# Infinity norm of 8192 rows: other load widths in the last eighth of the work

## The chip, the cores and the metric

The kernel runs on one core of a Trainium2 chip. The metric is the device time of one execution in microseconds (us). The kernel before took 626.63 us (median of three runs, 626.33 to 626.69).

## The reference

The input is a float32 matrix of 8192 rows and 8192 columns, 268.44 MB. The output is, for each row, the largest absolute value in it:

```
return np.linalg.norm(x, ord=np.inf, axis=1)
```

Every element is read once from HBM and compared once. Nothing else is computed.

## The kernel before

**Division of the work.** Each of the 128 partitions handles 64 whole rows. A *tile* is two rows for each partition: 128 x 16384 elements, 8.39 MB. A partition's two rows lie next to each other in HBM, so its 16384 elements are contiguous there. There are 32 tiles. The first 24 are the *bulk* (loop at L300 to L307): one load for each tile, issued on SyncE's queue at L303, and one reduction on VectorE, which gives both rows' maxima at once, into `r_bulk`. Three tile buffers (`BUFS=3`) rotate, so the load of a tile waits until VectorE has finished the tile three before it.

**The tail.** The last eight tiles are cut into several loads each, so that VectorE can start on a part of a tile as soon as that part has landed. `TAIL` (L18) holds the widths, in elements of a partition, of the loads of the first seven tail tiles; the loop at L309 to L320 issues them at L315. A reduction may not mix two rows, so `segments` (L39) cuts a load that crosses column 8192 of its tile into two reductions. Their results go to columns of `part`.

**The last tile.** `LAST` (L29) is the list of loads of the eighth tile, each a row (0 or 1) and a width, in the order of issue (L341). All but the last load of each row are reduced into single columns of the tile `t` itself, which stand just behind the place where that row's last load is put; the last reduction of a row reads its last load and these columns together, and writes `r_tail` (L345). After the first load of this list, one small reduction folds `part` into `r_tail` (L353).

**The end.** The store of `r_bulk` is issued on ScalarE's queue (L357) after the third-last load's reduction. The store of `r_tail` is issued on SyncE's queue (L359) behind the last reduction.

**Order and waits.** SyncE issues all loads in program order. A load waits for its buffer, as said. Loads also take turns on eight completion semaphores, so a load waits for the landing of the load eight before it where this isn't implied by its other wait. VectorE's reductions run in program order; each waits for its load's landing. All reductions show in the profile under line L296, the helper `absmax`.

**Sums of the widths.** Before, the seven tiles in `TAIL` are 20 loads and 26 reductions, and `LAST` is 12 loads and 12 reductions. With the small reduction over `part` that is 32 loads and 39 instructions on VectorE in the tail.

Of the kernel before, what the change touches and what calls it, by code (L numbers as in the profile page):

```python
# [15 lines left out]


TAIL = [  # L18
    [12672, 3712],
    [4992, 11392],  # L20
    [7040, 9344],
    [9344, 7040],
    [3584, 6784, 6016],
    [3968, 4224, 4736, 3456],
    [4096, 3584, 3200, 2944, 2560],
]


LAST = (  # L29
    [(0, w) for w in (2176, 1792, 1792, 1664)]  # L30
    + [(1, w) for w in (1664, 1408, 1280, 1152, 1024, 896)]
    + [(0, 768), (1, 768)]
)


# [359 lines left out]
```

## Time and profile before

| | |
|---|---|
| time, three runs | 626.33, 626.63, 626.69 us |
| the profiled execution | span 624.1 us, from the first load's issue to the end; the page gives no other time for it |
| median of the runs less this span | 2.5 us, outside the span |
| VectorE busy | 552.4 us, 89% of the span |
| DMA | 268.44 MB read, a mean of 430 GB/s |
| last tail load issued | 611.38 us after the span's start |
| last reduction ends, store of `r_tail` issued | 623.28 us, 623.31 us |

The profile is one execution on the chip. Its page names engines PE (TensorE), DVE (VectorE), ACT (ScalarE), POOL (GpSimd) and SP (SyncE); a trailing q means the engine's instruction queue, where DMAs are issued. The rows of instruction groups have busy time and the mean of one instruction in ns, then idle time just before them and what ended it. Consecutive reductions overlap by somewhat under 0.1 us in the records, so the time that one adds is read from start to start.

### The profile page before, as it was taken

To read this page: it belongs to the slowest core of one execution; us is meant where nothing else is said; L and a number is where in the kernel's file an instruction comes from. 1 tells how busy PE (TensorE), PEld (TensorE's weight loads), DVE (VectorE), ACT (ScalarE), POOL (GpSimd) and SP (SyncE) were. 2 spreads that over 40 slices of the span, in tenths; PEclk is the share of its full clock that TensorE was granted. 3 is DMA by queue.
4 is the path that set the end of the run, shared out by engine and by line. 5 is a ranking of instruction groups with operands and counts; after the bars stand their busy time and mean duration, and the time that the engine had idled before them with its cause. 6 is when DMAs were issued, how large, how long until landed. Compare 5 with 4: busy or idle time off the path is not lost.

```text
span 624.1 us, 151 instructions
## 1 busy us (share of the span) xinstructions
DVE 552.4 (89%) x63; POOL 0.3 (0%) x5
## 2 busy tenths in 40 slices
DVE  0688988889988899888898888988889999999999
POOL 0000000000000000000000000000000000000000
DMA  9999999999999999999999999999999999999998
GB/s 403 470 403 454 420 428 445 403 470 403 470 403 441 433 403 470 403 470 403 470 403 470 403 462 412 437 437 403 470 434 397 440 448 422 422 437 430 429 427 354
DMA packets 8593, 268.47 MB, mean 430 GB/s; under 512 B 1424, under 2 KB 1424, under 8 KB 2832
## 3 DMA queue, kind: packets, MB, share of 16 engines
q1 hardware_dynamic: 8064, 268.44, 99.7%
q10 hardware_dynamic: 528, 0.02, 0.1%
q14 instruction: 1, 0.01, 0.0%
HBM read 268.44 MB, written 0.03 MB: 430 GB/s over the span
## 4 chain that ended last, share of the span: by engine, by line
DMA 63%; DVE 36%; another core or an unknown queue 0%; DVEq 0%; issue 0%
DMA t<-in_x_dram 63%; DVE r_bulk L296 25%; DVE part L296 8%; DVE t L296 3%; DVEq L390 0%; DVE r_tail L296 0%
## 5 line engine op out<-in xcount | busy, mean ns | idle before, releaser
L296 DVE TENSOR_REDUCE r_bulk<-t 128x2 f32<-128x16384 f32 x24 | 413.3, 17220 | 70.6 <-DMA t<-in_x_dram 70.6
L296 DVE TENSOR_REDUCE part<-t 128x1 f32<-128x8192 f32 (+19 forms) x26 | 121.3, 4741 | 0.3
L296 DVE TENSOR_REDUCE t<-t 128x1 f32<-128x1792 f32 (+7 forms) x10 | 16.3, 1692 | 0.0
L296 DVE TENSOR_REDUCE r_tail<-t 128x1 f32<-128x772 f32 (+1 forms) x2 | 1.8, 948 | 0.0
L296 DVE TENSOR_REDUCE r_tail<-part 128x14 f32<-128x42 f32 x1 | 0.2, 192 | 0.0
L293 POOL MEMSET part<- 128x42 f32 x1 | 0.1, 133 | 0.0
L379 POOL MEMSET const-bfloat16-1.0<- 128x1 bf16 x1 | 0.1, 101 | 0.0
L379 POOL MEMSET const-uint8-127<- 128x1 uint8 x1 | 0.1, 101 | 0.0
L379 POOL MEMSET const-float32-0.0<- 128x1 f32 x1 | 0.1, 98 | 0.2 <-issue 0.2
L379 POOL MEMSET const-float32-1.0<- 128x1 f32 x1 | 0.1, 98 | 0.0
## 6 DMA issues: line engine op xcount, KB each, us to landing
t<-in_x_dram SPq DMA_DIRECT2D x2, 4672.0 KB, 37.5
t<-in_x_dram SPq DMA_DIRECT2D x2, 3520.0 KB, 36.2
t<-in_x_dram SPq DMA_DIRECT2D x1, 6336.0 KB, 36.3
t<-in_x_dram SPq DMA_DIRECT2D x1, 5696.0 KB, 40.5
t<-in_x_dram SPq DMA_DIRECT2D x2, 1792.0 KB, 34.3
t<-in_x_dram SPq DMA_DIRECT2D x1, 3392.0 KB, 37.5
t<-in_x_dram SPq DMA_DIRECT2D x1, 3008.0 KB, 44.2
t<-in_x_dram SPq DMA_DIRECT2D x1, 2496.0 KB, 27.3
```

The source lines that it names most:

```text
L293: nc.gpsimd.memset(part[:], 0.0)
L296: return nc.vector.reduce_max(out=o, in_=i, axis=X, apply_absolute_value=True)
L379: nc = _bacc.Bacc("TRN2", target_bir_lowering=False, num_devices=1)
```

## The change

Only the two lists of widths change. In `TAIL` the number of loads stays 20; two tiles are now cut at the end of a row (8192, 8192), and of the others five still have one load that crosses it, so the reductions go from 26 to 25. `LAST` has 11 loads instead of 12, wider at the start, with the rows in another order; its two final loads are 896 and 768 wide instead of 768 and 768. In all: 31 loads and 37 instructions on VectorE.

```
 TAIL = [
-    [12672, 3712],
-    [4992, 11392],
-    [7040, 9344],
-    [9344, 7040],
-    [3584, 6784, 6016],
-    [3968, 4224, 4736, 3456],
-    [4096, 3584, 3200, 2944, 2560],
+    [8192, 8192],
+    [12032, 4352],
+    [8192, 8192],
+    [7808, 8576],
+    [3584, 6272, 6528],
+    [5376, 4736, 3712, 2560],
+    [4096, 3712, 3200, 2688, 2688],
 ]

 LAST = (
-    [(0, w) for w in (2176, 1792, 1792, 1664)]
-    + [(1, w) for w in (1664, 1408, 1280, 1152, 1024, 896)]
-    + [(0, 768), (1, 768)]
+    [(0, 2432), (0, 2176), (1, 1920), (1, 1792), (0, 1536), (1, 1408)]
+    + [(1, 1280), (0, 1152), (1, 1024), (0, 896), (1, 768)]
 )
```

## The prediction

> **What bounds the kernel now.** I read the page first: engines, slices, groups.
>
> ```profile
> DVE 552.4 (89%) x63; POOL 0.3 (0%) x5
> DMA  9999999999999999999999999999999999999998
> ...
> L296 DVE TENSOR_REDUCE r_bulk<-t 128x2 f32<-128x16384 f32 x24 | 413.3, 17220 | 70.6 <-DMA t<-in_x_dram 70.6
> L296 DVE TENSOR_REDUCE part<-t 128x1 f32<-128x8192 f32 (+19 forms) x26 | 121.3, 4741 | 0.3
> ```
>
> The DMA engines are full from end to end. In the bulk, VectorE waits for every load (70.6 us in all); in the tail it hardly waits (0.3 us). That doesn't make VectorE the bound: it was given a backlog. So next come the busy times of two stretches, tail and bulk (length, VectorE busy, number of instructions), and the chain of waits in the tail (start, length, what).
>
> ```profile
> 466.66:622.20 155.54, 155.26 (x39) 0.00 (x0) 1.00 0.99 426
> 41.03:466.66 425.63, 378.83 (x22) 0.00 (x0) 1.00 1.00 433
> ```
>
> ```profile
> 501.18 34.55 DMA t<-in_x_dram
> 535.73 0.02 issue
> 535.75 17.35 DVE part L296 x3
> 553.10 0.02 issue
> 553.12 34.71 DMA t<-in_x_dram
> 587.83 0.02 issue
> 587.85 17.52 DVE part L296 x6
> 605.37 2.33 DVE t L296
> 607.70 0.10 DVE r_tail L296
> 607.80 13.50 DVE t L296 x9
> 621.30 0.17 issue
> 621.47 0.76 DVE r_tail L296
> ```
>
> VectorE is busy for 155.26 of 155.54 us, and twice the chain goes through a load that lands just as VectorE gets to it (535.73 and 587.83). So both are the bound at once. The last load is issued at 611.38 and takes 10.8 us to land (row of that load in the DMA issues): 622.2. The timeline shows the last reduction behind it:
>
> ```profile
> 621.47 1.81 DVE L296 TENSOR_REDUCE r_tail<-t 128x1 f32<-128x772 f32 x2
> 621.59 0.41 ACTq L357 DMA_DIRECT2D out_dram<-r_bulk  x1
> 623.31 0.35 SPq L359 DMA_DIRECT2D out_dram<-r_tail  x1
> ```
>
> The first of the pair starts at 621.47. An instruction of 772 elements takes 772/0.96 = 0.80 us and a fixed part of 0.06 (below), so the second starts at 622.34, about 0.15 after its load landed and with no gap behind the first. VectorE is the later of the two by 0.15 us. That is the most that any relief of VectorE can bring; beyond it the loads hold the end.
>
> **What a load costs.** The second and the 24th bulk reduction start 0.02 after their loads' landing, at 41.05 and 466.68: 425.63/22 = 19.35 us for a tile in one load. The eight tail tiles, in 32 loads, take 622.2 - 466.66 = 155.5; in eight loads they would take 154.8. So 24 extra loads cost 0.75 us, 0.03 each. One load less: -0.03 us, and the last landing is at about 622.15. Crossing a row's end costs the queue nothing: the 12672-wide load lands 14.9 after the one before (445.24 + 36.3 against 466.66), 1.18 ns an element, and the bulk load has 19.35/16384 = 1.18. So cutting at the row's end doesn't change the stream.
>
> **What a reduction costs.** By shape, 8192 elements take a mean of 8681 ns and 1152 take 1346: 7335/7040 = 1.042 ns an element and 146 ns fixed. Start to start it is less: the 8192-wide reduction that starts at 483.82 is followed by 4480 and 3712, and the next starts at 501.06: 17.24 us, of which 16384/0.96 = 17.07 is elements, so 0.06 fixed for each. Two instructions less (one in `part`, one in the last tile): -0.12 us of VectorE.
>
> **Where VectorE waits.** Loads' landings at the ends of the tail tiles are (issue plus time to landing) 486.0, 505.4, 524.7, 544.1, 563.5, 582.9, 602.4, 622.2. They stay, since the bytes do; inside a tile I place landings by 1.18 ns an element, and start each reduction at the later of landing and the end of the one before. Before, this gives waits of 0.20 at 535.7 (9344-wide), 0.25 at 587.8 (4096) and 0.04 at 613.4: 0.49. After:
> - Tile 0: 8192 lands at 476.3 and 486.0; VectorE, free at 483.82, takes them at 483.82 and 492.41, free at 501.00.
> - Tile 1: 12032 lands at 500.2, 0.8 ahead. Its 8192, 3840, and then 4352 end at 518.2. Tile 2: two of 8192, landed 3 and 2 us ahead, end at 535.4. The wait of 0.20 here is gone: 7808 landed at 533.9.
> - Tile 3: 7808 ends at 543.6, but 8576, which crosses the row's end, lands at 544.1: a wait of 0.50. Its 384 and 8192 end at 553.17; before, the tile ended at 553.00.
> - Tile 4 ends at 570.47 (6528 lands 0.16 ahead), tile 5 at 587.83, where 4096 lands within 0.02, as before. In tile 6 the 3712 makes it wait 0.08. It ends at 605.33; the 2432 of the last tile lands at 605.34.
> - Last tile: from 605.36 ten reductions with 15620 elements (16.27 us), their fixed parts (0.58) and the one over `part` (0.10) lie ahead of the last one. No load is later than VectorE by more than 0.01; the closest lands 0.03 ahead. The last reduction starts at 622.31 (before 622.34), 0.16 behind its landing. It has 773 elements instead of 774.
>
> So VectorE gains 0.12 from two instructions and loses 0.12 by waits (0.61 instead of 0.49), and the sum at the last reduction is between 0.00 and -0.03 us. The end of a wait in the trace is known to about 0.05, so each of the four close landings may cost that: -0.03 to +0.2.
>
> **Other edits.** The store of `r_bulk` now waits for the 1024-wide reduction instead of the 896-wide: its issue moves from 621.59 to about 621.4. It takes 2.4 us to land and the store of `r_tail` ends later (623.31 + 1.4 = 624.7), so this gives nothing, and 0.9 us of cover is left. The last reduction of row 0 now waits for VectorE's own result two instructions ahead (1152-wide; before, seven ahead). Nearest row: before, the last one of row 1 waited likewise two ahead, on the 896-wide, and started without a gap; so nothing, with the 0.10 us of the small reduction over `part` as the upper bound. SyncE's waits on the load eight before: before, the last load was issued with 8544 elements in flight (10.8 us); now it has 9856. The queue doesn't run dry.
>
> **The sum.** By the span: 624.1 - 0.03 = 624.1; with the 2.5 us outside it, against the median: 626.6 us.
>
> **Rivals.**
> *A load's fixed part is on the queue* (faster). The first load lands at 21.74 (its reduction starts at 21.76), 2.4 us more than the 19.35 of a tile. If each load paid that, one less would give 626.6 - 2.4 = 624.2. [...] Against it stand 24 extra tail loads that cost 0.03 each: the fixed part lies under the loads ahead. Chance 0.02.
> *VectorE catches up* (no change either): if all waits vanished, the end would be at the landing, 0.15 earlier, 626.5. Part of the forecast's range.
> *The wide loads of tiles 0 to 3 stream slower* (slower). Their row-wide loads have no row before. The nearest, 7040, takes 1.18 to 1.19 ns an element, the dearest of the tail (2560-wide) 1.21 with its fixed part. Eight loads of 65536 elements at 1.21 instead of 1.18 are +2.0 us: 628.6. Since no later tile has slack, all of it reaches the end; at +0.02 ns it exceeds 0.2%. Against it: bulk loads, wider still, run at 1.18. At the 1.19 of the nearest row it is +0.7: 627.3. Chance of over 0.2%: 0.04.
> *It doesn't do what it says*: five loads still cross a row's end, and one of these (8576) makes the longest wait. That is in the sum.
>
> **How the numbers follow.** A difference of 0.2% (1.25 us) is about what a measurement of this kernel can tell from no change. The forecast, 626.6 with chance 0.94, lies within it. The bulk itself scatters: the reductions' starts are 19.28 to 19.50 us apart, with four around 138 to 196 us that take 0.5 together over the usual; a run may have none or twice that, so 0.5 to either side. Add -0.15 (all waits gone) below and +0.2 (close landings) above: 625.9 to 627.3. The rivals beyond are under 2 in 10, so the range ends there. Faster 0.02, same 0.94, slower 0.04.
>
> **What would show it.** Right: the tail stretch again 155.5 us long with 37 instructions on VectorE; the chain through a load that lands at about 544.1 instead of 535.7; the last reduction 0.1 to 0.2 behind its landing. Wrong: a last landing off by more than 0.5 from 466.66 + 155.5, gaps on VectorE of over 1 us in the tail, or a last load that lands after VectorE is free.

## The result, and the profile after

The kernel after the change takes 627.50 us (median of 21 runs, 626.86 to 627.91), the kernel before 626.63 us (21 runs, 626.31 to 626.96). The ratio is 1.0013, 95% interval 1.0008 to 1.0019: 0.87 us slower by the medians, and outside the range that was given (625.9 to 627.3).

The page's lines of after that answer to those shown of before, and the busy times of the same two stretches, tail and bulk (in this execution the bulk went 0.5 us faster, so the tail begins at 466.13; columns as before: length, VectorE busy, number of instructions; the helper `absmax` is on L295 now):

```profile
DVE 552.3 (89%) x61; POOL 0.3 (0%) x5
DMA  9999999999999999999999999999999999999998
...
L295 DVE TENSOR_REDUCE r_bulk<-t 128x2 f32<-128x16384 f32 x24 | 413.3, 17220 | 70.1 <-DMA t<-in_x_dram 70.1
L295 DVE TENSOR_REDUCE part<-t 128x1 f32<-128x8192 f32 (+15 forms) x25 | 121.2, 4923 | 0.4 <-DMA t<-in_x_dram 0.4
```

```profile
466.13:621.65 155.52, 155.08 (x37) 0.00 (x0) 1.00 1.00 428
41.04:466.13 425.09, 378.83 (x22) 0.00 (x0) 1.00 1.00 433
```

The tail is as long as before: 155.52 against 155.54 us. Each stretch goes from the landing of the last bulk load to within 0.03 us of that of the last load. The chain of waits (start, length, what):

```profile
500.95 42.62 DMA t<-in_x_dram
543.58 0.02 issue
543.60 61.31 DVE part L295 x17
604.91 2.61 DVE t L295
607.52 0.10 DVE r_tail L295
607.62 13.12 DVE t L295 x8
620.74 0.08 issue
620.82 0.85 DVE r_tail L295
621.67 0.14 issue
621.82 0.95 DVE r_tail L295
```

It goes through the 8576-wide load, issued at 500.95, and VectorE waits for it until 543.60; from there it runs to the end. The last reduction starts at 621.82, 155.67 us after the 24th bulk reduction (466.15). Before, that was 155.66 (622.34 less 466.68). So nothing is lost inside the tail. The timeline of after, behind it:

```profile
620.82 1.94 DVE L295 TENSOR_REDUCE r_tail<-t 128x1 f32<-128x900 f32 x2
620.93 0.41 ACTq L356 DMA_DIRECT2D out_dram<-r_bulk  x1
622.79 0.35 SPq L358 DMA_DIRECT2D out_dram<-r_tail  x1
```

The last store is issued at once, at 622.79. The span of this execution is 623.53 us and its time 626.86: 3.33 us lie outside the span. Over the 21 runs, time less span is 3.50 us in the median; for before, in 33 runs with both numbers, it is 2.63. That is +0.87 us, the whole loss, and it stands where the span doesn't see it: the last store counts to the span with its issue only (622.79), while it lands at 624.91, behind the span's end. The rows of the DMA issues, first before, then after (size, us to landing):

```profile
out_dram<-r_tail SPq DMA_DIRECT2D x1, 8.0 KB, 1.4
```

```profile
out_dram<-r_tail SPq DMA_DIRECT2D x1, 8.0 KB, 2.1
```

The same 8 KB store lands 0.7 us later after its issue. What lies beside it shows in the DMA view of narrow stretches. Before, from 622.4 to 623 (queue, packets, share of the 16 engines in this stretch), and from 624.1 to 624.5, where the store's packets are, in 40 slices:

```profile
q10 hardware_dynamic: 510, 0.02, 53.5%
q14 instruction: 1, 0.01, 4.5%
```

```profile
DMA  0000002376659466556334111000000000000000
...
q1 hardware_dynamic: 144, 0.01, 23.1%
```

And after, from 623.4 to 624.1, in 40 slices of 17.5 ns:

```profile
DMA  0090000000000046755544211000000000000010
GB/s 0 0 468 0 0 0 0 0 0 0 0 0 0 7 51 66 66 45 44 48 40 34 22 11 8 0 0 0 0 0 0 0 0 0 0 0 7 7 11 4
...
q1 hardware_dynamic: 144, 0.01, 13.3%
q14 instruction: 1, 0.01, 5.4%
```

The profile calls the kind of queue q14 "instruction" and shows one packet of 8192 bytes on it here. I read it as a fetch of instructions for an engine, by the queue's name alone: the trace shows neither what the packet holds nor which engine it is for. Such a packet is called a *fetch* below. Before, it came at 622.47, between the last load and the last store, beside the store of `r_bulk` (q10), which has time to spare (it lands at 624.00, the store of `r_tail` at 624.73). After, it starts in the third slice, 623.44, and takes 5.4% of 16 engines in 0.7 us, so one engine for 0.60 us, until 624.04. In that time the store's 144 packets arrive (128 of 64 bytes and 16 of 4 bytes). Most go through in one group, slices 14 to 25; a rest of nine packets, a sixteenth of 144, waits until the 37th slice, 624.03, which is when the fetch ends. So the rest looks like the share of the engine that the fetch holds; the trace does not name the engine. The group is 0.2 us wide before and 0.46 with this rest. That is 0.26 of the 0.70 us; the other 0.44 pass between the last packet and the landing (0.36 us before, 0.80 after).

### The profile page after: what moved, and what is told of

Read it like the earlier page. It is cut to its first block, busy times and chain, and to the rows that moved or that the text cites. A ratio compares the mean times of both kernels' runs of the same rounds, so it can differ in the third digit from the quotient of the medians.

```text
span 623.5 us, 148 instructions
## 1 busy us (share of the span) xinstructions
DVE 552.3 (89%) x61; POOL 0.3 (0%) x5
## 4 chain that ended last, share of the span: by engine, by line
DMA 59%; DVE 40%; another core or an unknown queue 0%; issue 0%; SPq 0%
DMA t<-in_x_dram 59%; DVE r_bulk L295 25%; DVE part L295 13%; DVE t L295 3%; DVE r_tail L295 0%; SPq L314 0%
## 5 line engine op out<-in xcount | busy, mean ns | idle before, releaser
L295 DVE TENSOR_REDUCE r_bulk<-t 128x2 f32<-128x16384 f32 x24 | 413.3, 17220 | 70.1 <-DMA t<-in_x_dram 70.1
L295 DVE TENSOR_REDUCE part<-t 128x1 f32<-128x8192 f32 (+15 forms) x25 | 121.2, 4923 | 0.4 <-DMA t<-in_x_dram 0.4
L295 DVE TENSOR_REDUCE t<-t 128x1 f32<-128x2432 f32 (+8 forms) x9 | 16.0, 1846 | 0.0
L295 DVE TENSOR_REDUCE r_tail<-t 128x1 f32<-128x900 f32 (+1 forms) x2 | 1.9, 1013 | 0.0
L295 DVE TENSOR_REDUCE r_tail<-part 128x14 f32<-128x42 f32 x1 | 0.2, 186 | 0.0
```

Source lines behind the costliest of these rows:

```text
L295: return nc.vector.reduce_max(out=o, in_=i, axis=X, apply_absolute_value=True)
```

## The experiments

Theory A: the fetch is VectorE's; it is set off when VectorE reaches a fixed place of its program, and two instructions less put that place later in time, into the last store. Theory B: one load less moves the stores on SyncE's queue and to other completion semaphores. Theory C: the widths cost it. The kernels ran in three groups on three chips, where before took 626.5, 627.0 and 626.9, so ratios compare within a group, and time less span compares everywhere (before: 2.63 to 2.65 in all three).

**Two instructions given back to VectorE.** Small reductions into an unused tile, in the bulk, where VectorE waits 2.05 to 2.17 us for each load but the first (profile of after):

```
+            if 0 < a * G + n <= 2:
+                j = a * G + n
+                absmax(spare[:, j : j + 1], t[:, :8])
```

> After, with two additional 8-element reductions on VectorE behind the second and third bulk reductions (results in an unused tile), so that VectorE has as many instructions as before; loads and widths are those of after. Theory A (an 8192-byte instruction fetch, which VectorE's place in its program sets off, now runs into the last store): the fetch moves back to about 1.6 us before the end of the span, the store of r_tail lands 1.4 us after its issue instead of 2.2, time less span 2.5 us, median 626.6 (626.3 to 626.8). Theory B (the stores' place on SyncE's queue and their semaphores, moved by the one load less): 627.5, time less span 3.5. Theory C (the widths themselves): 627.5.

Measured: 626.45 us, ratio 0.9999 (0.9990 to 1.0008), time less span 2.63. The DMA view from 622.1 to 622.8 has the fetch, and the store lands as before:

```profile
DMA  0009046779999597687777868663200000000010
...
q14 instruction: 1, 0.01, 5.3%
```

```profile
out_dram<-r_tail SPq DMA_DIRECT2D x1, 8.0 KB, 1.4
```

The fourth of 40 slices is 622.17, 0.92 us before the store's issue (623.09). All widths and loads are those of after, with the 8576-wide load's wait of 0.50, and the cost is gone. Against theories B and C.

**One DMA given back to SyncE.** A load of 8 elements into the unused tile, in the bulk:

```
+            if 0 < a * G + n <= 1:
+                j = 8 * (a * G + n)
+                nc.sync.dma_start(out=spare[:, j : j + 8], in_=x_b[a, n][:, :8])
```

> After, with one additional load of 8 elements per partition on SyncE's queue behind the second bulk load (into an unused tile), so that SyncE issues as many DMAs as before and the stores use the same semaphores as before; VectorE's instructions and the widths are those of after. Theory A (VectorE's instruction fetch): nothing changes, 627.5 (the small load may add up to 0.1), time less span 3.5. Theory B (SyncE's queue and semaphores): 626.6, time less span 2.5. Theory C (widths): 627.5.

Measured: 627.30, ratio 1.0013 (1.0004 to 1.0021), time less span 3.50, and the store's row:

```profile
out_dram<-r_tail SPq DMA_DIRECT2D x1, 8.0 KB, 2.2
```

Theory B falls.

**Before, with two instructions less on VectorE.**

```
-                absmax(part[:, i * B + b, k : k + 1], t[:, lo : lo + n])
+                if n not in (512, 1152) or i == 3:
+                    absmax(part[:, i * B + b, k : k + 1], t[:, lo : lo + n])
```

> Before, without two small reductions of the tail (the 1152-wide one of the third tail tile and the 512-wide one of the seventh; their columns of part stay zero), so that VectorE has two instructions less, as after; all loads are those of before. VectorE has 1.9 us less work in the tail, which can bring up to 0.15 us (the last landing then sets the end). Theory A: the fetch moves to where it is in after, the store of r_tail lands 2.2 us after its issue, 627.3 (627.1 to 627.5). Theories B and C: 626.5, time less span 2.5.

Measured: 627.60, ratio 1.0017 (1.0008 to 1.0026), time less span 3.50. The store's row and the DMA view from 623.8 to 624.6:

```profile
out_dram<-r_tail SPq DMA_DIRECT2D x1, 8.0 KB, 2.1
```

```profile
DMA  0000090000000000000266555441100000011000
...
q14 instruction: 1, 0.01, 4.6%
```

The fetch, the group and the late rest are those of after, with before's lists: the cost of the change made without the change. Half of the expectation missed: 1.9 us less work on VectorE brought none of the 0.15 us. The last reduction starts 155.65 us after the 24th bulk reduction. VectorE's starts show longer waits instead, 1.45 at 535.78, 0.53 at 599.40 and the last at 613.40, from where the same loads and reductions as before lead to the end.

**Each list alone.**

> The lists TAIL of after with LAST of before: 32 loads, 38 instructions on VectorE, one less than before. Theory A: the fetch lies between its places in before and after, about 0.5 to 1 us later than before; if it ends before the last store's packets start, 626.6, if it runs into them, up to 627.5. Theory B: 626.6 (SyncE's queue is that of before). Theory C: 627.5 if the cost is in the widths of TAIL, 626.6 if it is in those of LAST.

Measured: 627.25, ratio 1.0012 (1.0003 to 1.0021); time less span 2.97, store in 1.7 us, so 0.3 us is in the store. Another 0.37 is inside: the last reduction starts 156.03 after the 24th bulk reduction instead of 155.66.

> The list LAST of after with TAIL of before: 31 loads, 38 instructions on VectorE. Theory A (the number of VectorE's instructions places the fetch): as in the two other kernels with 38, the fetch starts about 0.25 us after the last store's issue, the store lands in 1.7 to 2.0 us, the last reduction comes 0.3 us later than in after, and the ratio to before is 1.0008 to 1.0015. Rival (one of the two lists carries the cost by its widths; TAIL alone cost 0.75 us): 1.0000.

Measured: ratio 1.0013 (1.0004 to 1.0022), time less span 3.32, store in 2.2 us, the last reduction 0.31 late without a landing as the reason. Half of the expectation missed: the fetch starts 0.72 us after the store's issue, not 0.25, and the store lands later than forecast. (In the profiled execution the loads too land 0.5 us later in the tail, from the second tail load on.) Each list alone costs as much as both: the cost isn't a sum over widths.

**One instruction given back.**

> After, with one additional 8-element reduction on VectorE behind the second bulk reduction: 38 instructions that count, as in the run with TAIL alone, but with the widths and loads of after. Theory A (VectorE's place in its program sets off the fetch): the fetch starts about 0.3 us after the issue of the last store, as in the run with TAIL alone, and runs partly into it: the store lands in 1.4 to 1.8 us, time less span 2.7 to 3.1, median 626.6 to 627.0. Rival (the cost with one instruction less is that of the list LAST of before, in that run): 626.5.

Measured: ratio 1.0011 (1.0002 to 1.0020), time less span 3.35, store in 2.0 us. The fetch is where it was expected (+0.25), but the store is dearer than forecast: TAIL alone, with the fetch at the same place, has 1.7 us. So the start of the fetch alone does not set the size of the delay. The rival (LAST of before) falls, since here LAST is that of after. The timeline of this kernel shows the other part:

```profile
621.08 1.08 DVE L295 TENSOR_REDUCE r_tail<-t 128x1 f32<-128x900 f32 x1
621.19 0.41 ACTq L359 DMA_DIRECT2D out_dram<-r_bulk  x1
622.39 0.96 DVE L295 TENSOR_REDUCE r_tail<-t 128x1 f32<-128x773 f32 x1 [0.23 <-DVE r_tail L295]
623.37 0.35 SPq L361 DMA_DIRECT2D out_dram<-r_tail  x1
```

VectorE stands idle for 0.23 us before the last reduction, 0.32 from start to start beyond its work, though the last load landed at 621.86.

**More instructions, and fewer.** Three, four and eight additional reductions in after, one in before, and four left out of after:

> After, with three additional 8-element reductions in the bulk: 40 instructions that count, one more than before. With 39 the fetch came with the last reduction (622.2), with 41 at 586.6. Theory A with a fixed place in the program: the fetch is one instruction earlier than with 39, at about 621 to 622, behind or among the last loads. If it goes in steps of several instructions instead: at 587 to 592, and the load under way then lands up to 0.5 later. Store in 1.4 us and time less span 2.6 either way; ratio to before 0.9998 to 1.0008.

> Before, with one additional 8-element reduction in the bulk: 40 instructions on VectorE, with the widths and loads of before. Theory A: the fetch is where it is in after with three additional ones (621 to 622, or 587 to 592), whatever the widths; store in 1.4 us, time less span 2.6; ratio to before 0.9998 to 1.0008. If the fetch hung on SyncE or the widths, it would stay at 622.5 and the ratio at 1.0000.

> After, with four additional 8-element reductions in the bulk (two more instructions on VectorE than before). Theory A: the fetch comes some 2 us earlier than before, at about 620 to 621, while the last loads still stream; store in 1.4 us, time less span 2.6. The 8192 bytes take one DMA engine of 16 about 0.3 to 0.6 us, so the last landing may come that much later: 626.4 to 626.9.

> After, with eight additional 8-element reductions in the bulk (six more instructions on VectorE than before). Theory A: the fetch comes at about 614 to 616 in the stream of loads; store in 1.4 us, time less span 2.6; the last landing up to 0.5 later than in after, or not, if the engine catches up: 626.4 to 626.9.

> After, without four small reductions of the tail (both 384-wide ones, the 1664-wide and the 1920-wide one, whose columns of part stay zero): VectorE has four instructions less than after. Theory A: VectorE does not reach the place that sets off the fetch before its program's end, so no fetch runs into the last store: the store lands in 1.4 us. The fetch then comes later, in what follows: 626.5 if nothing waits for it, up to 627.3 if the end does. Rival (fewer instructions on VectorE is dearer in itself): more than 627.5.

All, by VectorE's instructions that count (39 before, 37 after); the fetch's start against the last store's issue, and the store's landing after its issue, are those of the profiled execution:

| kernel | instructions | fetch | store lands | time less span | ratio to before |
|---|---|---|---|---|---|
| after, four left out | 33 | +3.5 us | 1.4 us | 3.07 us | 1.0001 |
| after | 37 | +0.65 | 2.1 | 3.50 | 1.0013 |
| after, one small load more | 37 | +0.90 | 2.2 | 3.50 | 1.0013 |
| before, two left out | 37 | +0.57 | 2.1 | 3.50 | 1.0017 |
| TAIL alone | 38 | +0.26 | 1.7 | 2.97 | 1.0012 |
| after, one more | 38 | +0.25 | 2.0 | 3.35 | 1.0011 |
| LAST alone | 38 | +0.72 | 2.2 | 3.32 | 1.0013 |
| before | 39 | -0.84 | 1.4 | 2.63 | |
| after, two more | 39 | -0.92 | 1.4 | 2.63 | 0.9999 |
| after, three more | 40 | -1.17 | 1.4 | 2.64 | 1.0001 |
| before, one more | 40 | -1.20 | 1.4 | 2.61 | 1.0002 |
| after, four more | 41 | -37.4 | 1.4 | 2.62 | 1.0002 |
| after, eight more | 45 | -49.7 | 1.4 | 2.62 | 1.0003 |

The table's fourth and fifth columns can be compared in one execution, since the profiled execution of each kernel but before has its own time on record. There the time less span exceeds 2.63 us by 0.70, 0.83, 0.69, 0.30, 0.61 and 0.74 us in the six kernels with 37 and 38, in the table's order, and the store lands later than in before by 0.70, 0.83, 0.69, 0.30, 0.60 and 0.74. With 39 to 45 both differences are under 0.01; with 33 they are 0.40 and 0.00. So from 37 up the late landing of the last store is all that is added outside the span.

The fetch comes earlier with more instructions on VectorE, with either pair of lists, though not by one fixed step: with 37 it lies between +0.57 and +0.90, with 38 at +0.25, +0.26 and +0.72. At 37 and 38 it meets the last store; at 39 and 40 it falls into the gap between the last load and the last store; at 33 it comes after the store. There the store lands in 1.4 us again, but the time outside the span is 0.42 longer than that of before in this group (3.07 against 2.65), with the fetch at 626.75 as the only DMA in its stretch:

```profile
q14 instruction: 1, 0.01, 1.0%
```

That the end waits for it there is inferred. It may also be another packet than in the other kernels: this one takes five packets of 8192 bytes on q14 in the 12 us before the span, all others six. Its ratio, 1.0001 (0.9992 to 1.0010), doesn't tell a cost. At 41 and 45 the fetch is among the loads: with 41 it starts at 586.55, a landing that VectorE waits for then comes 0.5 us late (a wait of 0.53 at 588.49), and the last reduction starts 156.20 us after the 24th bulk one, though the ratio (1.0002, 0.9993 to 1.0011) is not told from 1. With 45 the landing behind the fetch is 0.5 us late too. Loads come late by as much without a fetch (LAST alone), so that the fetch is the cause here is not shown. My expectation for 41 and 45 (620 to 621, and 614 to 616) was wrong: two instructions more than 39 move the fetch by 36 us, then four more by 13. The forecast for 40 missed by less: the fetch is at 622.87 and 622.74, not at 621 to 622, and at the same distance from the store with either pair of lists. Counting VectorE's reductions from the start of the program (the 24 of the bulk and the additional ones too) up to the fetch gives, with 41 and with 45:

```profile
0.00:586.55 586.55, 515.69 (x47) 0.27 (x5) 1.00 1.00 432
0.00:573.88 573.88, 503.45 (x47) 0.27 (x5) 1.00 1.00 432
```

It is the 47th reduction in both. With 39 and 40 the fetch starts in the 63rd, in all four kernels. That fits places counted in VectorE's program, as in Theory A, but there is more than one, and why it changes between 40 and 41 is open. No kernel tried beats before.

## Why the prediction was wrong

- **The tail, right.** 31 loads and 37 instructions leave the stream as long (155.5 expected, 155.52 measured), the wait of 0.50 at the 8576-wide load is 0.51, the last reduction starts 0.19 behind its landing at 621.63 (0.16 expected) and -0.03 to +0.2 from before's place (measured +0.01). The fixed costs of a load (0.03) and of a reduction (0.06) fit this. One number of the working is off without effect: before, the last eight loads, in flight when the last is issued, are 8960 elements and not 8544.
- **The step that failed** is the last line of the sum: "with the 2.5 us outside it". I took what lies outside the span as a constant, and in "Other edits" the store of `r_tail` as ending 1.4 us after its issue. Time less span is 2.63 before and 3.50 after, and 626.6 + 0.87 = 627.5 is the measured time. The term left out is the fetch: in the six kernels where it starts 0.25 to 0.90 us after the last store's issue, that store lands in 1.7 to 2.2 us (after: 2.1), in the seven others in 1.4. Two instructions given back to VectorE undo it (after with two more: 1.4), a load given back to SyncE doesn't (2.2). I priced it at nothing because I did not look at what the DMA engines do between the last load and the end. It was there to see: one packet on q14 in the page of before, and in its narrow stretch at 622.47.
- **The rivals** were about the load stream and VectorE's waits; none was about the end. The slower one (wide loads stream slower) did not happen: 8192-wide loads land 9.65 to 9.67 us apart, 1.18 ns an element. A load's fixed part on the queue did not show either: with one load less the tail is 155.52 us long, against 155.54 before. Slower had a chance of 0.04 for over 0.2%; the 0.13% measured is within the 0.94, but above the range.
- **The gain from VectorE** was put at up to 0.15 us. With 1.9 us less work the end didn't move at all: the waits come back, the last at 613.40. Less work behind that wait was not tried, so whether the 0.15 can be had there is not shown.

## What to carry to other kernels

Where the last DMA of a kernel is short, price it by its landing and not by its issue, and look at everything that runs on the DMA engines in the last microseconds, instruction queues too: here the same 8 KB store landed 1.4 us after its issue in seven kernels and 1.7 to 2.2 us after it in the six where the fetch met it. Two instructions less on VectorE moved the fetch from 0.84 us before that store's issue (before) to 0.65 us after it (after). If a variant with other widths moves the time by under 1 us, test a few idle instructions more or less before the widths are believed. Time less span is a sharper measure of such an end than the time: its medians of before agreed within 0.02 us on three chips, where its times differ by 0.5.

## What the runs showed of the hardware that I had not expected

- The packet of 8192 bytes on q14 takes 0.43 us in before, 0.60 in after, 0.30 in after with one small load more and 0.76 in after with one more (the last two by its share of 16 engines). In the six kernels where it meets the last store, that store lands 0.30 to 0.83 us later than in before. In after the last packets are only 0.27 us late (624.10 against 623.83 for the others), but of the 16 semaphore updates that make up the store's landing the last comes 0.70 us after the other 15 (624.91 against 624.21). In TAIL alone and in after with one more, no packet of the store is late: the last ends 1.05 and 1.07 us after the issue (before, 1.06), and the landing is 0.30 and 0.60 late all the same. Why the landing is later than the packets is open.
- With 38 instructions VectorE makes a pause of 0.31 to 0.32 us before the last reduction (three kernels), with 40 one of 0.32 to 0.37 before the last but one (two kernels), with 33, 37, 39, 41 and 45 neither. Each of these two reductions has a separate wait instruction before it, so both are the same place counted from the program's start. With 37 the instruction at that place is the drain behind the last reduction, and it starts 0.51 to 0.53 us after the wait ahead of that reduction, against 0.10 to 0.11 with 33, 39, 40, 41 and 45. So a pause at a fixed place fits all three counts. What VectorE waits for there is open: with 38 and 40 the packet on q14 starts only 0.65 to 1.7 us after the pause has ended, so it isn't this packet.
